# A hybrid encoder step whose inputs arrive in another host layout: key cache and memory tokens turned, weights contiguous per partition, states returned as they lie on chip

## The chip, the cores and the metric

The kernel runs on one core of a Trainium2 chip. TensorE (PE in the profile) multiplies, VectorE (DVE) and ScalarE (ACT) do the elementwise work, GpSimd (POOL) and SyncE (SP) issue most of the transfers. The metric is the device time of one execution in microseconds, lower is better.

## The reference, cut to what matters

One layer, fp32. A prompt of 512 positions and 8 cached samples of 16 positions (128 rows) go through the same weights.

```python
z = x @ w_in                       # [RG-LRU input | its gate | GLU | query | 3 branch gates]
xa_c = causal_depthwise_conv([conv_a_prev, xa])              # width 4
h, h_last = rg_lru(xa_c, h_prev, ...)                        # scan over positions
out_a = (h * gelu(ya)) @ proj_a
u = glu[..., :D_CONV] * sigmoid(glu[..., D_CONV:])
v = causal_depthwise_conv([conv_b_prev, u])                  # width 31
out_b = silu(layer_norm(v)) @ proj_b
out_c = mem_cross_attention(q, k, v) @ proj_c                # 4 heads, 256 memory tokens
merged = g0 * out_a + g1 * out_b + g2 * out_c
x = layer_norm(ALPHA * x + merged @ w_out)
x = layer_norm(ALPHA * x + swiglu(x))
```

For the prompt, `k` and `v` are `mem_prompt @ w_mem_k` and `mem_prompt @ w_mem_v`; for the samples they come from `cache_mem_k` and `cache_mem_v`. Besides the two results the kernel returns the new convolution and recurrence states and the new memory keys and values.

## The kernel before

All 640 rows are kept on chip with the model dimension on partitions (`xh`, `xl`), in two halves of 320 columns. Every fp32 product is made of three fp32r matmuls: each operand is split into a rounded high part and a low part, and high by high, high by low and low by high are summed. A weight block is loaded by SP into `wr` (1 MB, two buffers), ACT copies it to `wh` (high), DVE writes `wl` (low), and PE multiplies.

The program is a list of `Step`s in the order in which PE does them: keys and values of the memory tokens, GLU, query, RG-LRU input, gates and projections of branches C and B, RG-LRU gate, the gates of branch A (`Pair`, seven half-size products instead of eight, with the sums made on DVE and ACT), branch A's projection, `w_out`, the FFN and its down projection. Weights are prepared up to three steps ahead.

Between a step's matmuls the program advances `streams`: generators for the work beside the projections (attention, the convolutions, the recurrence). A stream goes on while the summed prices of DVE and ACT (`V.time`, `A.time`) are below that of PE (`P.time`), so the place of a stream's instructions follows from a table of prices; `finish` forces a stream to its end where a step needs it. The stream that multiplies the recurrence by its gate is `a_stream`; it copies each product to a rounded part on ACT and subtracts on DVE. Small tiles live in 52 slots (`s`), side results in two PSUM buffers (`pv`), projection sums in four (`pu`).

What the change touches before: `mem_turn` transposes the memory tokens on PE. `load_rows` loads 14 small arrays as rows, and `param_stream` turns them on PE into `pa` and `pb` (a parameter for each channel, on partitions) and the sample histories into `us`. `conv_b_states` turns the new state of convolution B back into rows, the end of `lru_stream` does it for `hout`. In `attn_sample`, `turn` transposes each of the 16 key cache tiles in eight blocks of eight, and ACT copies the result to `kt` for `scores`. Weight blocks are read with rows of 1 to 4 KB, a strided slice of the model's matrix. Nearly all compute instructions stand on line 64 in the profile, the line of the helper that records them; tile names tell them apart. Only the loop that runs the steps and the streams is needed to follow the order:

```python
for few in s.mm(s.w):
    ...
    advance()
    flush()
    while new:
        new.pop(0).prep_lo()
```

## Time and profile before

| | |
|---|---|
| median of three runs | 1083.74 us (1081.05 to 1085.24) |
| span of the profiled execution | 1078.8 us; the page has no device time of its own for it |
| PE / DVE / ACT / POOL busy | 98% / 74% / 44% / 10% |
| mean granted TensorE clock | 0.996 |
| read from and written to HBM | 112.41 MB, 9.61 MB |

A line of the page's groups gives engine, operation, result and operands by tile name, count, busy time and the mean of one; a row of the timeline gives start, length and the like, with the idle time of the engine just before it and what ended it in brackets. Matmuls are pipelined, so the length of a row on PE is longer than the time to the next start.

### The profile page before, as it was taken

The page shows a single profiled execution, that of the slowest core. Times are in us where ns is not written, and L with a number is a line of the kernel's source. Part 1 is how long each engine was busy: PE and PEld are TensorE (multiplying, and loading weights), DVE is VectorE, ACT ScalarE, POOL GpSimd, SP SyncE. Part 2 cuts the span into 40 slices and gives each one's busy share as a digit, 9 for nine tenths or more (in the row PEclk, how much of TensorE's full clock was granted, in tenths as well). Part 3 has the DMA queues.
Part 4 walks back from the last instruction along what each step waited for, and adds up shares of the span by engine and source line. Part 5 has one row for each costly group of instructions (what it writes and reads, how often), then busy time and mean ns, then how long its engine had stood idle before and what let it go on. Part 6 is the DMA issues. An engine that isn't in the chain of part 4 may idle for free.

```text
span 1078.8 us, 16991 instructions
## 1 busy us (share of the span) xinstructions
PE 1052.7 (98%) x6827; PEld 1002.7 (93%) x6827; DVE 798.6 (74%) x1357; ACT 479.4 (44%) x852; POOL 107.8 (10%) x158
## 2 busy tenths in 40 slices
PE   9799999999999999999999998999999999999997
PEld 8699999998999999999999888999999999888886
DVE  6939989988377747877545678888878887545775
ACT  5332655455584575455323024434444444343341
POOL 0300405325000000100001220000000000100111
PEclk9999999999999999999999999999999999999999
DMA  9822124625022122113326231222232222834481
GB/s 337 276 87 73 46 79 141 200 83 157 1 90 88 59 84 93 45 53 105 118 72 221 98 118 40 78 79 78 83 110 82 79 79 79 293 122 152 159 289 40
DMA packets 80334, 123.11 MB, mean 114 GB/s; under 512 B 4075, under 2 KB 59371, under 8 KB 80256
## 3 DMA queue, kind: packets, MB, share of 16 engines
q1 hardware_dynamic: 73168, 100.36, 28.3%
q0 software_dynamic: 7088, 21.68, 6.4%
q8 instruction: 53, 0.87, 0.3%
q14 instruction: 25, 0.20, 0.1%
HBM read 112.41 MB, written 9.61 MB: 113 GB/s over the span
## 4 chain that ended last, share of the span: by engine, by line
PE 54%; DVE 1%; ACT 0%; issue 0%; DVEq 0%; ACTq 0%
PE pu L64 48%; PE pv L64 6%; DVE s L64 1%; DVE xres L64 0%; ACT s L64 0%; ACT wh L64 0%; DVEq L1952 0%; ACT wl L64 0%; DVE st L64 0%; DVE mv L64 0%; DVE ve L64 0%; DVE wl L64 0%; ACTq L64 0%; DVEq L64 0%
## 5 line engine op out<-in xcount | busy, mean ns | idle before, releaser
L64 PE MATMUL pu<-xh,wh 128*128 128x320 f32 x1040 | 250.2, 313 | 7.4 <-ACT s L64 6.8
L64 PE MATMUL pu<-xh,wl 128*128 128x320 f32 x1040 | 245.9, 309 | 0.0
L64 ACT ACTIVATE wh<-wr 128x1024 fp32r<-128x1024 f32 (+1 forms) x149 | 135.2, 909 | 222.6 <-PE pu L64 137.7
L64 PE MATMUL pu<-xl,wh 128*128 128x320 f32 x888 | 218.9, 310 | 4.1 <-DVE xl L64 4.1
L64 PEld LDWEIGHTS pu<-xh,wh 128*128 128x128 f32 x1040 | 177.2, 189 | 11.0 <-ACT s L64 7.8
L64 PE MATMUL pu<-s,wh 128*128 128x320 f32 x1064 | 185.5, 310 | 0.9 <-DVE s L64 0.9
L64 PEld LDWEIGHTS pu<-xh,wl 128*128 128x128 f32 x1040 | 176.8, 188 | 0.0
L64 DVE TENSOR_TENSOR wl<-wr,wh 128x1024 fp32r<-128x1024 f32 (+1 forms) x113 | 130.1, 1152 | 62.6 <-ACT wh L64 62.5
L64 DVE TENSOR_TENSOR s<-s,s 128x640 fp32r<-128x640 f32 (+4 forms) x176 | 126.1, 733 | 66.9 <-ACT s L64 64.6
L64 PEld LDWEIGHTS pu<-s,wh 128*128 128x128 f32 x1064 | 163.4, 188 | 2.2 <-DVE s L64 2.0
L64 PEld LDWEIGHTS pu<-xl,wh 128*128 128x128 f32 x888 | 153.5, 188 | 4.7 <-DVE xl L64 4.7
L64 DVE TENSOR_TENSOR s<-s,pu 128x320 f32<-128x320 f32 x188 | 88.5, 485 | 84.5 <-PE pu L64 81.7
L64 PE MATMUL pu<-s,wl 128*128 128x320 f32 x808 | 147.0, 309 | 0.0
L64 ACT ACTIVATE s<-s 128x640 fp32r<-128x640 f32 (+4 forms) x144 | 87.7, 628 | 100.1 <-DVE s L64 99.5
L64 PEld LDWEIGHTS pu<-s,wl 128*128 128x128 f32 x808 | 126.0, 188 | 0.0
L64 PE MATMUL pu<-wh,s 128*128 128x512 f32 (+1 forms) x396 | 115.4, 383 | 0.1
L64 DVE SCALAR_TENSOR_TENSOR s<-s,pb,s 128x511 f32<-128x511 f32 (+14 forms) x240 | 112.6, 540 | 2.8 <-ACT s L64 2.8
L64 PEld LDWEIGHTS pu<-wh,s 128*128 128x128 f32 x396 | 72.5, 188 | 14.6 <-ACT wh L64 0.9
L64 ACT ACTIVATE s<-pu 128x320 f32<-128x320 f32 (+2 forms) x90 | 36.8, 444 | 66.9 <-PE pu L64 66.7
L64 PE MATMUL pu<-wl,s 128*128 128x512 f32 (+1 forms) x198 | 61.6, 383 | 1.9 <-DVE wl L64 1.9
L64 PE MATMUL pv<-wh,s 128*128 128x512 f32 (+1 forms) x152 | 48.7, 367 | 0.4 <-DVE xres L64 0.4
L64 PE MATMUL pv<-s,s 128*32 128x128 f32 (+4 forms) x420 | 45.8, 308 | 1.4 <-ACT s L64 1.4
(134 smaller groups left out, 1172.6 us busy)
## 6 DMA issues: line engine op xcount, KB each, us to landing
wr<-in_w_in SPq DMA_DIRECT2D x26, 1024.0 KB, 5.0
wr<-in_w_ffn_down SPq DMA_DIRECT2D x19, 1024.0 KB, 4.9
wr<-in_w_ffn_gate SPq DMA_DIRECT2D x11, 1024.0 KB, 5.3
wr<-in_w_ffn_up SPq DMA_DIRECT2D x11, 1024.0 KB, 5.4
s<-in_cache_mem_k POOLq DMA_DIRECT2D x16, 256.0 KB, 5.9
s<-in_cache_mem_v POOLq DMA_DIRECT2D x16, 256.0 KB, 4.5
wr<-in_proj_a SPq DMA_DIRECT2D x4, 1024.0 KB
wr<-in_w_out SPq DMA_DIRECT2D x4, 1024.0 KB, 5.8
```

The costliest lines, as they stand in the source:

```text
L64: return f(*a, **k)
```

## The change

The host lays out the arrays before they go to the device, and lays the results out again after it:

- Memory tokens arrive turned, in four tiles `[128, 2, 256]`; `mem_split` only splits them. 30 matmuls of the identity stand ahead of the first real one in place of 15.
- Parameters and small states arrive as `rows_a` and `rows_b`, already on partitions, and are loaded into `pa` and `pb`. The sample histories arrive as `hist_b`, with 16 empty columns, straight into `us`.
- The key cache arrives as `[head, 128, tokens]`, the value cache as one contiguous row for each partition; two heads of keys are loaded ahead.
- Weights arrive so that a block is one contiguous row for each partition.
- `us`, the last 30 columns of `up` and `hout` are stored as they lie on chip.

```diff
-def mem_turn(c):
-    p = pv()
-    for m in range(2):
-        for k in range(4):
-            P.transpose(p[:, m, k * 128:(k + 1) * 128], mem[m][c][:, k * 128:(k + 1) * 128], ident)
...
+def mem_split(i):
+    hi, lo = memT[i] = [get([128, 2, 256], F32R) for _ in range(2)]
+    split(hi, lo, mem[i])
+    free(mem[i])
...
-idle(5)
-mem_turn(0)
-idle(10)
+idle(15)
+mem_split(0)
+idle(15)
...
 def load_rows():
...
+    S.dma_start(pa, rows_a.rearrange("p (k r) -> p k r", k=KD))
+    S.dma_start(pb, rows_b.rearrange("p (k r) -> p k r", k=KC))
+        S.dma_start(us[k], hist_b[k].rearrange("p (b r) -> p b r", b=NB))
...
 def z_load(col, n=1):
...
-        zload[c] = Load([128, KD, 256],
-                        lambda c=c: w_in[:, c:c + 256].rearrange("(k p) n -> p k n", p=128), 2)
+        zload[c] = Load([128, 2, KD, 128],
+                        lambda c=c: blocks_of(w_in[c // 256], 2), 2)
...
 def conv_b_stream():
...
+        G.dma_start(state_b[k].rearrange("p (b r) -> p b r", b=NB), us[k])
+        G.dma_start(tail_b[k], up[k][:, TP - 30:TP])
         yield from conv_b_taps(k)
-        free(us[k])
...
-            yield from conv_b_states()
...
+        free(us[k], up[k])
...
 def attn_sample():
...
-            to[h] = [get([128, 4, 128]) for _ in range(4)]
-            rows = src[0].rearrange("b (m p) h d -> p (b m) h d", p=128)
+            to[h] = [get([128, 512]) for _ in range(4)]
             for i in range(4):
-                G.dma_start(to[h][i], rows[:, 4 * i:4 * i + 4, h])
+                G.dma_start(to[h][i], src[h][:, i * 512:(i + 1) * 512])
...
-        def turn(h, i):
...
-                    P.transpose(p[:, j, k * 128:(k + 1) * 128], kc[h][2 * i + j][:, k], ident)
...
+        for h in range(2):
+            load(kc, cache_k, h)
         yield None
         yield None
-        yield from room(2)
+        yield from room()
         acc = pv()
...
+        for h in range(NH):
+            yield None
+            scores(h)
+            if h + 2 < NH:
+                load(kc, cache_k, h + 2)
+            if h == NH - 1:
+                load(vc, cache_v, 0)
+            yield 1
...
 def lru_stream():
...
-            P.transpose(p[:36, j // 4, (j % 4) * 128:(j % 4 + 1) * 128], hout[:, j], ident)
...
+        G.dma_start(state_a.rearrange("p (k r) -> p k r", k=KD), hout)
```

The order of instructions changes at three places of note.

In the cached attention, PE's rows at the second head before: `ident` marks a transpose, `s_125` and `s_126` are tiles of the key cache, `s_129` to `s_132` turned copies, `s_95` the query.

```order
L64 MATMUL pu<-xl,wh 128x320 x2
L64 MATMUL pu<-xh,wl 128x320 x2
L64 MATMUL pv<-ident,s_125_2204 128x128 x4
L64 MATMUL pv<-ident,s_126_2205 128x128 x4
L64 MATMUL pv<-s_129_2249,s_95_1771 32x256
L64 MATMUL pv<-s_130_2251,s_95_1771 32x256
L64 MATMUL pv<-s_132_2302,s_95_1771 32x256
```

PE at the first head's scores now, with `s_113` to `s_116` tiles of the cache as loaded and `s_91` the query:

```order
L64 MATMUL pu<-xl,wh 128x320 x2
L64 MATMUL pu<-xh,wl 128x320 x2
L64 MATMUL pv<-s_113_2073,s_91_1756 32x256
L64 MATMUL pv<-s_114_2074,s_91_1756 32x256
L64 MATMUL pv<-s_115_2075,s_91_1756 32x256
L64 MATMUL pv<-s_116_2076,s_91_1756 32x256
```

The transposes are gone, and the scores read the loaded tile.

PE's first rows before, at the start of the program; `s_1` and `s_3` are memory tokens, `s_31` and `s_33` their rounded turned copies.

```order
L64 MATMUL pu<-ident 128x128 x5
L64 MATMUL pv<-ident,s_1_93 128x128 x4
L64 MATMUL pv<-ident,s_3_95 128x128 x4
L64 MATMUL pu<-ident 128x128 x10
L64 MATMUL pu<-wh,s_31_169 128x512
L64 MATMUL pu<-wh,s_33_173 128x512
```

PE's first rows now, with `s_31` and `s_41` rounded memory tiles and `s_32` a low part:

```order
L64 MATMUL pu<-ident 128x128 x30
L64 MATMUL pu<-wh,s_31_170 128x512 x4
L64 MATMUL pu<-wl,s_31_170 128x512 x4
L64 MATMUL pu<-wh,s_32_171 128x512 x4
L64 MATMUL pu<-wh,s_41_248 128x512 x4
```

Eight transposes ahead of the first real matmul and eight behind its step are gone; 15 identity matmuls have come.

DVE in the seven-product part of branch A's gates before; `wh<-` and `wl<-` are low halves of weights (both halves of a product's weights share a tile there), `s_320` and the like are sums of products.

```order
L64 TENSOR_TENSOR s_320_5251<-s_320_5251,pu 128x320
L64 TENSOR_TENSOR wh<-wr,wh 128x512
L64 TENSOR_TENSOR wl<-wr,wl 128x512
L64 TENSOR_TENSOR s_321_5252<-s_320_5251,pu 128x320
L64 TENSOR_TENSOR s_326_5293<-s_321_5252,pu 128x320
```

DVE at the same place now, where `s_248` is a rounded product of the recurrence with its gate and `s_251` the gate of the next one:

```order
L64 TENSOR_TENSOR s_282_5025<-s_282_5025,pu 128x320
L64 TENSOR_TENSOR wh<-wr,wh 128x512
L64 TENSOR_TENSOR s_249_4545<-s_183_3019,s_248_4544 128x640
L64 TENSOR_TENSOR wl<-wr,wl 128x512
L64 TENSOR_TENSOR s_189_3112<-s_189_3112,s_251_4581 128x640
```

Rows of `a_stream`, which stood ahead of this part, stand inside it; in all there are 14 of them up to the projection of branch A.

## The prediction

> **What bounds the kernel now.** I read the page's busy times first, then the busy times of stretches, then what TensorE (PE) waited for.

> ```profile
> PE 1052.7 (98%) x6827; PEld 1002.7 (93%) x6827; DVE 798.6 (74%) x1357; ACT 479.4 (44%) x852; POOL 107.8 (10%) x158
> PE 54%; DVE 1%; ACT 0%; issue 0%; DVEq 0%; ACTq 0%
> ...
> 21.10:38.00 16.90, 13.93 (x67) 10.55 (x66) 16.08 (x29) 8.78 (x15) 1.89 (x2) 1.00 0.82 271
> 38.00:56.50 18.50, 13.41 (x91) 12.37 (x89) 15.72 (x26) 5.24 (x9) 7.20 (x10) 1.00 0.85 283
> ...
> 62.80:160.00 97.20, 97.20 (x686) 97.18 (x685) 83.03 (x171) 45.30 (x113) 10.93 (x24) 1.00 0.22 71
> ...
> 191.80:230.70 38.90, 38.90 (x306) 36.41 (x304) 38.20 (x79) 19.89 (x43) 8.44 (x12) 1.00 0.58 173
> ...
> 477.00:527.00 50.00, 49.26 (x335) 49.26 (x336) 36.17 (x62) 27.27 (x49) 0.00 (x0) 1.00 0.31 97
> ```

> Each stretch gives its length and then the busy time of PE, weight loads, DVE, ACT and POOL. PE is busy for 98% of the span, and the share is not an average of unlike stages: from 62.8 to 160 it is 97.20 of 97.20. Only the opening differs. From 21.1 to 38 DVE is the full engine (16.08 of 16.90) and PE idles 3 us; from 38 to 56.5 PE idles 5.1. At 191.8 both are full; at 477 DVE has room.

> ```profile
> PE pu L64 <- ACT s L64: 6.8, 3, 4.3
> PE pu L64 <- DVE xl L64: 4.1, 2, 3.3
> PE pu L64 <- DVE wl L64: 1.9, 1, 1.9
> ...
> PE pv L64 <- DVE xl L64: 0.3, 1, 0.3
> 30.77 1.34 PE L64 MATMUL pu<-wl,s 128*128 128x512 f32 x4 [1.85 <-DVE wl L64]
> 41.66 0.42 PE L64 MATMUL pu<-xl,wh 128*128 128x320 f32 x1 [3.33 <-DVE xl L64]
> ```

> These are the first three and the last of the ten releasers that PE waited for; all ten are DVE or ACT, none a transfer. So a faster weight load by itself is worth nothing in PE's dense part, and an instruction taken off PE there is worth its spacing, as long as DVE and ACT keep up.

> **The change part by part: key cache.** 64 PE transposes go, and 16 ACT copies with them.

> ```profile
> 191.86 1.03 PE L64 MATMUL pv<-ident,s 128*128 128x128 f32 x8
> 192.65 0.54 PE L64 MATMUL pu<-xh,wh 128*128 128x320 f32 x2
> ...
> 195.96 0.45 PE L64 MATMUL pu<-xh,wl 128*128 128x320 f32 x2
> 196.25 1.04 PE L64 MATMUL pv<-ident,s 128*128 128x128 f32 x8
> 200.65 0.60 PE L64 MATMUL pv<-ident,s 128*128 128x128 f32 x4
> ```

> Between two blocks of eight transposes stand 24 projection matmuls. Their last pair takes 0.29 (195.96 to 196.25), 0.147 each, so 24 take 3.52; the blocks start 4.39 apart (191.86 to 196.25). A block therefore costs 0.87, or 0.109 a transpose. Eight blocks: **7.0 us**.

> PE's score matmuls now read the loaded tile itself (first pair of orders in the part on the change).

> **Parameter rows, histories and states.** 32 more transposes go from the dense part.

> ```profile
> 58.04 0.31 PE L64 MATMUL pu<-xh,wl 128*128 128x320 f32 x1
> 58.19 1.63 PE L64 MATMUL pv<-ident,s 86*128 86x86 f32 x8
> ...
> 60.00 0.31 PE L64 MATMUL pu<-xl,wh 128*128 128x320 f32 x1
> ...
> 61.46 0.32 PE L64 MATMUL pu<-xh,wl 128*128 128x320 f32 x1
> 61.62 0.99 PE L64 MATMUL pv<-ident,s 120*128 120x120 f32 x8
> ...
> 62.60 0.31 PE L64 MATMUL pu<-xl,wh 128*128 128x320 f32 x1
> L64 PE MATMUL pv<-ident,s 128*30 128x128 f32 x4 | 0.9, 273 | 0.0
> L64 PE MATMUL pv<-ident,hout x8: 270/272/273, 432.6 to 433.4; 128*36 128x128 f32 x8
> ```

> The row that is left out before 60.00 is one matmul, so 58.04 to 60.00 holds two spacings (0.29) and the parameter block: 1.67. 61.46 to 62.60 gives 0.85 for the convolution histories. The state rows of convolution B (4 of 30 columns and 4 of 128) are 8 transposes, those of `hout` another 8 at the same spacing (432.6 to 433.4 from first to last): 0.87 each. Together 4.3, and with the keys **11.2 us**. The 15 ACT copies and 25 small stores that go with them lie on engines with room (ACT 44%); the larger state stores run beside PE. Cost: nothing; if POOL's queue were needed at that moment, 0.5 to 0.75 an issue.

> **The opening.** 16 memory transposes go, 15 idle matmuls (two records each) come.

> ```profile
> 1.44 2.50 PE L64 MATMUL pu<-ident 128*128 128x128 f32 x10 [1.44 <-DVE ident L64]
> 3.74 1.91 PE L64 MATMUL pv<-ident,s 128*128 128x128 f32 x8
> 5.45 2.71 PE L64 MATMUL pu<-ident 128*128 128x128 f32 x20
> 8.21 1.26 PE L64 MATMUL pu<-wh,s 128*128 128x512 f32 x4
> ```

> By the second pair of orders, 60 records stand where 38 stood; 22 more at 0.109 put the first real matmul 2.4 later, near 10.6, and the second memory block gives 0.87 back. That is 1.5 late on PE, against 3.0 us in which PE waited for DVE from 21.1 to 38 and 5.1 after it. DVE's rows there are the same splits and norms in the same order, so the wait shrinks and the end stays: 0. The weight blocks arrive in longer rows now, and the DMA engines are busy for 0.82 and 0.85 of these two stretches; a transfer that lands earlier can only help where DVE stands idle, which is 0.82 (16.90 - 16.08) and 2.78 (18.50 - 15.72), 3.6 in all, and DVE's idle time there may as well be for ACT. Bounds: a loss of 2.4, or a gain of 0.87 and half of PE's 8.1 us of idle time (about the 3.6 of DVE); I take 0, nearest to the full DVE row.

> **Layout alone.** Contiguous rows for weights and values, two heads of keys ahead, and the histories with 16 empty columns change when a transfer lands, and no row of an engine. Behind the opening I cost them at nothing: what hides them is PE's own work, since no transfer is among its releasers, and at 62.8 to 160 the DMA engines are busy for 0.22, at 191.8 for 0.58. The histories and parameters are needed from 58 on, where the removed transposes read them; were they late, the convolution's stream would give its place to others and PE would go on. If that cover were gone, the price would be that of a late load (below, 4.4 each).

> **What is late next.** The scheduler fills DVE and ACT by its sum of PE time, which is now smaller, so recurrence work moves to later steps. In the gates of branch A, the part with seven products in place of eight (trace from 477), DVE now has rows of the recurrence between the low halves of the weights that PE waits for (third pair of orders). 14 such 128x640 rows moved into the 28 products.

> ```profile
> L64 DVE TENSOR_TENSOR s<-s,s 128x640 f32<-128x640 f32 x56 | 45.9, 820 | 1.7 <-ACT s L64 0.7
> L64 ACT ACTIVATE s<-s 128x640 fp32r<-128x640 f32 x64 | 46.3, 730 | 54.8 <-DVE s L64 54.8
> 476.11 0.74 ACT L64 ACTIVATE s<-s 128x640 fp32r<-128x640 f32 x1 [1.73 <-DVE s L64]
> 477.27 0.42 ACT L64 ACTIVATE s<-pu 128x320 f32<-128x320 f32 x1
> 477.74 0.42 PE L64 MATMUL pu<-xh,wh 128*128 128x320 f32 x1 [1.81 <-ACT s L64]
> ```

> 14 x 0.82 = 11.5 on top of 36.17 makes DVE 47.7 of 50 there: nearly full, not over. At 477 PE already waited 1.81, because ACT's evacuation stood behind a copy that waited for DVE. The last scans of the recurrence now stand just ahead of that place. New waits: between 0 and 6 (seven products of the recurrence, each holding DVE for an ACT copy of 0.73, is 5.1, and 1 at the entry); I take 2.

> **Sum.** 1078.8 - 11.2 + 2 = 1069.6 span. The page gives no device time for its execution; the median of the runs, 1083.74, lies 4.9 above the span, and I keep that: **1074.5**.

> [...] The durations here are alike (270 to 273 ns), but the rows at 191.86 show the starts 0.109 apart, and the spacing decides.

> **Rivals.**
> *DVE takes PE's place* in the seven-product part: all of the 6 us of new waits, and 1 to 2 more where DVE was full at 191.8. For it: 38.20 of 38.90 there. Against it: DVE's lead over PE.

> ```profile
> 198.10 1.21 DVE L64 TENSOR_TENSOR wl<-wr,wh 128x1024 fp32r<-128x1024 f32 x1
> 210.64 1.03 PE L64 MATMUL pv<-ident,s 128*128 128x128 f32 x8
> ```

> Counted in DVE's order, the row at 198.10 is the low half for the projection step that PE begins behind the block at 210.64. It is done at 199.3, 11 us ahead. Time: 1083.74 - 11.2 + 7.5 = 1080.

> *The opening shortens too*, since the memory tiles no longer pass through PE: half of the 8.1 us. Time: 1074.5 - 4 = 1070.5. Against it: DVE's 16.08 of 16.90.

> *A transpose holds PE for its whole duration*: 96 x 0.273 = 26.2, so 1057.5. The rows at 191.86 speak against it.

> *Slower: PE stands in front of a load.* Before, an ACT copy lay between the key tile and PE.

> ```profile
> L1066 POOL DMA_DIRECT2D s<-in_cache_mem_k x16: 749/749/806, 178.4 to 190.8; - x16
> DMA to landing us min/median/max: 3.4/5.9/8.4
> ```

> Heads 2 and 3 of keys and values are issued two rounds ahead, 2 x 3.52 = 7.0. Four issues of 0.75 and the longest landing make 11.4. If POOL came to the load only then, each would be 4.4 late, 17.6 for four, and the time 1083.74 - 11.2 + 17.6 = 1090. It decides once slots come free less than 11.4 before use. Against it: POOL had issued all keys by 190.8, before the first turn.

> That the change doesn't remove the transposes is excluded by the order's rows.

> **How the numbers follow.** Forecast 0.62 (own range 1071.5 to 1077.5), DVE 0.20, opening 0.12, whole durations 0.02, slower 0.04. A measurement of this kernel tells about 0.5% (5.4 us) from no change, so faster means under 1078.3: the forecast, the opening, the whole durations and a third of the DVE case, 0.82; within, the rest of that case, 0.14; slower 0.04. The range 1069.5 to 1080.5 leaves out the ends of the opening case, half of DVE's and both far ones.

> **What would show it.** Right: blocks gone from 58 and from 190 to 230; no new releaser over 3 us; the end of the opening near 56.5 still released by DVE. Wrong: PE waits with `wh` or `wl` from DVE between the gate projection's start and the branch A projection (the DVE case); PE releasers named after the caches (slower); first projection matmul well before 38 (opening).

## The result, and the profile after

| | before | changed |
|---|---|---|
| median | 1082.53 us (1081.05 to 1085.24, 4 runs) | 1073.88 us (1072.94 to 1074.25, 4 runs) |
| ratio | | 0.9916, 95% interval 0.99 to 0.9932 |
| span of the profiled execution | 1078.8 us | 1072.1 us |
| granted clock, mean | 0.996 | 0.991 |

The kernel became 8.65 us faster; the forecast was 1074.5. The lines below show that the forecast's largest term holds, and that its smaller ones are not those that made up the sum.

The page of the changed kernel, then the busy times of the same stretches (length, then PE, weight loads, DVE, ACT, POOL, and then the granted clock):

```profile
PE 1047.4 (98%) x6745; PEld 998.4 (93%) x6745; DVE 798.8 (75%) x1357; ACT 469.1 (44%) x823; POOL 89.5 (8%) x142
38.00:56.50 18.50, 15.43 (x88) 14.95 (x88) 13.75 (x22) 3.35 (x6) 1.86 (x2) 0.82 0.53 174
62.80:160.00 97.20, 94.75 (x654) 94.33 (x653) 78.93 (x157) 41.56 (x98) 10.58 (x30) 0.98 0.23 79
191.80:230.70 38.90, 38.66 (x320) 34.76 (x319) 32.01 (x65) 17.58 (x45) 7.79 (x15) 1.00 0.43 146
477.00:527.00 50.00, 50.00 (x342) 49.90 (x341) 43.62 (x71) 28.49 (x49) 0.00 (x0) 1.00 0.30 106
```

PE is busy 5.3 us less (1052.7 to 1047.4), where 11.2 were to go. Two clocks are new: 0.82 from 38 to 56.5 and 0.98 from 62.8 to 160, where before had 1.00. From 62.8 to 160 PE now also idles 2.45. At 477, where new waits were forecast, PE has none (50.00 of 50.00). From 191.8 on DVE, nearly full before (38.20 of 38.90), has 32.01 now. What PE waited for, and two places in its timeline:

```profile
PE pu L64 <- ACT s L64: 8.0, 5, 4.3
PE pu L64 <- DVE xl L64: 4.2, 2, 3.4
...
36.14 0.31 PE L64 MATMUL pu<-xh,wh 128*128 128x320 f32 x1
39.81 0.63 PE L64 MATMUL pu<-xl,wh 128*128 128x320 f32 x1 [3.35 <-DVE xl L64]
40.24 0.47 PE L64 MATMUL pu<-xh,wl 128*128 128x320 f32 x1
40.50 0.47 PE L64 MATMUL pu<-xh,wh 128*128 128x320 f32 x1
...
45.57 0.31 PE L64 MATMUL pu<-xl,wh 128*128 128x320 f32 x1
...
127.01 0.46 PE L64 MATMUL pu<-xh,wl 128*128 128x320 f32 x2
129.92 0.74 PE L64 MATMUL pu<-xh,wh 128*128 128x320 f32 x2 [2.45 <-ACT s L64]
```

The wait for `xl` ends at 39.81, 1.85 earlier than before (41.66). But the matmuls behind it start 0.26 apart until 45.57, and 0.15 apart from there. The granted clock of that stretch is 0.50, called half speed here, as these windows of both profiled executions show, first the changed kernel's, then before's:

```profile
35.30:38.72 3.42, 1.15 (x6) 0.69 (x4) 3.35 (x6) 2.60 (x5) 1.48 (x1) 1.00 0.79 302
38.73:42.14 3.41, 2.33 (x9) 2.34 (x10) 3.41 (x6) 0.45 (x1) 0.00 (x0) 0.50 0.53 113
42.14:45.55 3.41, 3.41 (x14) 3.41 (x14) 3.27 (x6) 0.00 (x0) 0.00 (x0) 0.50 0.97 318
127.47:130.88 3.41, 0.96 (x5) 0.82 (x6) 3.41 (x8) 3.38 (x8) 0.00 (x0) 1.00 0.00 0
130.89:134.29 3.40, 3.40 (x15) 3.40 (x14) 3.40 (x8) 1.83 (x5) 0.00 (x0) 0.50 0.00 0
666.78:670.19 3.41, 2.62 (x10) 2.62 (x11) 3.38 (x6) 1.78 (x4) 0.00 (x0) 0.50 0.00 0
670.20:673.60 3.40, 3.40 (x14) 3.40 (x14) 2.27 (x4) 1.99 (x4) 0.00 (x0) 0.50 0.00 0
...
36.80:40.21 3.41, 1.53 (x8) 0.98 (x6) 3.34 (x7) 2.21 (x5) 1.41 (x1) 1.00 0.92 291
40.22:43.62 3.40, 1.96 (x13) 1.96 (x14) 3.40 (x6) 0.84 (x1) 0.05 (x1) 1.00 0.78 277
675.10:678.50 3.40, 3.40 (x13) 3.40 (x14) 3.37 (x6) 0.92 (x2) 0.00 (x0) 0.50 0.00 0
```

The windows are 3.41 us long because the stretches at 0.50 are, once (130.89 to 134.29, and 675.10 to 678.50 before) or twice (38.73 to 45.55, 666.78 to 673.60). The place of before's first two is an estimate, 186 steps of 3.413 back from 675.10. In the changed kernel PE was busy for 1.15 of the window up to 38.72 and 0.96 of the one up to 130.88, and the window behind each has 0.50. Before, nearly the same wait (3.33) lies in two windows (PE busy 1.53 and 1.96), and the clock there is 1.00. Half of PE's busy time in windows at 0.50 is counted as lost: (2.33 + 3.41 + 3.40 + 2.62 + 3.40)/2 = 7.6 us now, 1.7 before. The starts give somewhat less: from 40.24 to 45.57 they lie 0.267 apart in place of 0.147, which makes the lost share 0.45.

This gives an account of the two profiled executions. Span: -6.7. PE's idle time: 26.1 (1078.8 - 1052.7) to 24.7, -1.4. Lost to half speed: +5.9. What is left, PE's work at full speed, is -6.7 + 1.4 - 5.9 = **-11.2** (the start, ahead of the clock's first record, counted as full speed). A second pair of executions, before_again and after_again below (spans 1080.7 and 1070.0), gives -10.7 + 1.8 - 0.4 = -9.3. Both hold the identity matmuls of the opening, which the term of 11.2 did not count. Counted from the first projection matmul on (38.03 before, 36.14 now), PE's work at full speed fell by 11.3 in the first pair and by 10.2 in the second: the term holds within about a microsecond.

### The profile page after: what moved, and what is told of

It is laid out like the page before. It is cut to its first block, busy times and chain, and to the rows that moved or that the text cites. A ratio compares the mean times of both kernels' runs of the same rounds, so it can differ in the third digit from the quotient of the medians.

```text
span 1072.1 us, 16734 instructions
## 1 busy us (share of the span) xinstructions
PE 1047.4 (98%) x6745; PEld 998.4 (93%) x6745; DVE 798.8 (75%) x1357; ACT 469.1 (44%) x823; POOL 89.5 (8%) x142
## 4 chain that ended last, share of the span: by engine, by line
PE 83%; DVE 10%; DMA 3%; ACT 2%; issue 1%; POOL 0%; SPq 0%; DVEq 0%; POOLq 0%; ACTq 0%
PE pu L64 74%; PE pv L64 10%; DVE s L64 7%; DVE wl L64 2%; ACT s L64 1%; DMA s<-in_w_mem_k 1%; DMA pb<-in_rows_b 1%; DMA s<-in_x_prompt 1%; DMA s<-in_w_mem_v 1%; DVE xres L64 0%; DVE xl L64 0%; ACT L64 0%; DVE mx L64 0%; POOL s L777 0%; DVE nm L64 0%
## 5 line engine op out<-in xcount | busy, mean ns | idle before, releaser
L64 PE MATMUL pu<-xh,wh 128*128 128x320 f32 x1040 | 251.7, 314 | 8.3 <-ACT s L64 7.5
L64 PE MATMUL pu<-xh,wl 128*128 128x320 f32 x1040 | 247.6, 310 | 0.0
L64 ACT ACTIVATE wh<-wr 128x1024 fp32r<-128x1024 f32 (+1 forms) x149 | 135.1, 908 | 242.2 <-PE pu L64 152.4
L64 PE MATMUL pu<-xl,wh 128*128 128x320 f32 x888 | 220.6, 312 | 4.2 <-DVE xl L64 4.2
L64 PEld LDWEIGHTS pu<-xh,wh 128*128 128x128 f32 x1040 | 178.8, 190 | 12.9 <-ACT s L64 9.2
L64 PE MATMUL pu<-s,wh 128*128 128x320 f32 x1064 | 185.6, 310 | 1.7 <-DVE s L64 1.3
L64 DVE TENSOR_TENSOR s<-s,s 128x640 fp32r<-128x640 f32 (+4 forms) x180 | 129.0, 732 | 67.3 <-ACT s L64 60.7
L64 PEld LDWEIGHTS pu<-xh,wl 128*128 128x128 f32 x1040 | 178.2, 189 | 0.0
L64 DVE TENSOR_TENSOR wl<-wr,wh 128x1024 fp32r<-128x1024 f32 (+1 forms) x113 | 129.9, 1151 | 62.9 <-ACT wh L64 62.7
L64 PEld LDWEIGHTS pu<-s,wh 128*128 128x128 f32 x1064 | 163.1, 188 | 3.3 <-ACT wh L64 1.1
L64 PEld LDWEIGHTS pu<-xl,wh 128*128 128x128 f32 x888 | 155.1, 190 | 4.8 <-DVE xl L64 4.7
L64 PE MATMUL pu<-s,wl 128*128 128x320 f32 x808 | 148.1, 311 | 0.2 <-DVE s L64 0.2
L64 DVE TENSOR_TENSOR s<-s,pu 128x320 f32<-128x320 f32 x188 | 88.5, 485 | 75.0 <-PE pu L64 71.4
L64 ACT ACTIVATE s<-s 128x640 fp32r<-128x640 f32 (+4 forms) x148 | 89.8, 627 | 99.0 <-DVE s L64 97.6
L64 PEld LDWEIGHTS pu<-s,wl 128*128 128x128 f32 x808 | 126.8, 190 | 0.5 <-ACT wh L64 0.5
L64 DVE SCALAR_TENSOR_TENSOR s<-s,pb,s 128x511 f32<-128x511 f32 (+14 forms) x240 | 114.5, 549 | 9.5 <-ACT s L64 9.4
L64 PE MATMUL pu<-wh,s 128*128 128x512 f32 (+1 forms) x396 | 114.8, 383 | 0.0
L64 PEld LDWEIGHTS pu<-wh,s 128*128 128x128 f32 x396 | 72.8, 188 | 13.9
L64 ACT ACTIVATE s<-pu 128x320 f32<-128x320 f32 (+2 forms) x90 | 36.6, 441 | 71.9 <-PE pu L64 71.9
L64 PE MATMUL pu<-wl,s 128*128 128x512 f32 (+1 forms) x198 | 61.6, 383 | 0.4 <-DVE wl L64 0.4
L64 PE MATMUL pv<-wh,s 128*128 128x512 f32 (+1 forms) x152 | 48.7, 367 | 0.4 <-DVE xres L64 0.4
L64 PE MATMUL pu<-s,s 128*128 128x512 f32 (+1 forms) x204 | 46.6, 380 | 0.0
```

What stands on the lines that cost most here:

```text
L64: return f(*a, **k)
```

## The experiments

All medians are beside runs of the kernel before on the same chip (medians 1083.07, 1083.19 and 1083.38 in the three sets).

| label | median, us | ratio to before, 95% interval |
|---|---|---|
| before_again | 1084.43 | 1.0013 (1.0004 to 1.0022) |
| after_again | 1074.03 | 0.9919 (0.9905 to 0.9933) |
| warm_both | 1070.40 | 0.9887 (0.9874 to 0.9901) |
| credit | 1066.35 | 0.9846 (0.9833 to 0.986) |
| credit_warm | 1062.51 | 0.9804 (0.979 to 0.9819) |
| keys_on_chip | 1079.89 | 0.9966 (0.9954 to 0.9978) |
| params_on_chip | 1071.32 | 0.9892 (0.9876 to 0.9908) |
| mem_on_chip | 1075.14 | 0.9933 (0.9917 to 0.9949) |
| idle15 | 1074.54 | 0.9916 (0.9901 to 0.993) |
| strided | 1074.08 | 0.9914 (0.9897 to 0.993) |
| keys_only | 1078.60 | 0.996 (0.9945 to 0.9975) |
| before_warm | 1081.68 | 0.9983 (0.997 to 0.9995) |

The first row is a kernel against itself, and its interval leaves out 1: 0.0013 is what such a ratio can be off, beyond its interval.

### Does half speed follow from the program, or from the run?

Both kernels were run once more, unedited, to choose between two accounts: in the one, called the clock theory in the expectations, the windows at 0.50 stand at other places in other runs of the same program; in its rival the program alone sets them.

> The kernel before, once more. [...] Rival (the windows follow from the program alone): every run at 0.996, and the half-speed stretches stand again at 675 and at the end only.

> The changed kernel, once more. Clock theory: 1072.5 to 1074.5, granted clock 0.991 to 0.995, the half-speed stretches not all at the same places as in the first profile (38.7, 130.9, 666.8). Rival (they follow from the program): the same three places, clock 0.991 in every run. By both the waits of 3.35 at 39.8, 2.45 at 129.9 and 4.32 at 667.6 stand again within 0.2 us.

The second execution of before, with the windows around its first wait and around the one at 477:

```profile
39.23:42.62 3.39, 1.14 (x8) 1.14 (x9) 3.39 (x6) 1.62 (x3) 0.86 (x1) 1.00 0.92 334
42.64:46.03 3.39, 3.39 (x14) 3.39 (x14) 3.25 (x5) 0.00 (x0) 0.00 (x0) 0.50 0.96 245
476.13:479.53 3.40, 1.58 (x11) 1.32 (x10) 3.20 (x6) 2.57 (x5) 0.00 (x0) 1.00 0.00 0
479.54:482.95 3.41, 3.41 (x15) 3.41 (x14) 3.32 (x6) 1.51 (x3) 0.00 (x0) 0.50 0.02 5
```

The same program, but the windows meet at another place (42.63, where 40.22 was estimated for the first execution), and here the one behind 1.14 of 3.39 busy has 0.50; at 477 one behind 1.58 of 3.40, 1.82 idle, has it too. So the program alone does not set the places, and the profile of before that the forecast was made from (clock 0.996) had less half speed than most: of the 54 runs of before in the three sets and in before_again, five have 0.996 or more. Of the 15 runs of before beside this set, the two at clock 0.997 took 1080.52 and 1081.24, the four at 0.992 that took longest 1083.07 to 1084.63. The changed kernel's nine runs all lie at 0.991 or 0.992, 0.9917 in the mean, before's fifteen 0.9935. 0.0018 of 1075 us, or some 2 us, is an estimate of what half speed takes back from the change on the average; with the mean of all 54 runs of before, 0.9929, it is 1.3. The first pair had 5.9, the second 0.4 (5.1 lost in before_again, 5.5 in after_again). A run of 1082.32 at 0.992 says that the mean clock alone does not set the time; the mean also takes in windows in which PE waits (busy for 2.33 of 3.41 at 38.73 in the changed kernel).

after_again came out nearer to the rival than to the clock theory. Its waits are the same (3.33, 2.43 and 4.32), its half-speed stretches follow the same three waits (from 39.52, 128.26 and 664.16), and no run left 0.991 to 0.992. Only the places of the windows differ: PE is busy for 3.03 and 2.90 of the first two half-speed windows, where it was busy for 2.33 of 3.41 and 3.40 of 3.40. So the mean clock of the changed kernel hardly differs between runs, and it is before's that does (0.992 to 0.997 in the fifteen). That waits of this length (2.43 to 4.32) are followed by half speed in most runs is the author's reading of these rows, not a test.

### Idle matmuls in the waits

The first loop stands ahead of the first projection step, the second ahead of the first seven-product step of the FFN. Both write a PSUM buffer that the next real product overwrites, and their price is not counted, so that the order stays.

```diff
+    for _ in range(14):
+        nc.tensor.matmul(q.p[0][:, :128], ident, ident, start=True, stop=True)
...
+    for _ in range(18):
+        nc.tensor.matmul(q[:, 0, :128], ident, ident, start=True, stop=True)
```

> 14 identity matmuls ahead of the first projection step and 18 ahead of the first seven-product step of the FFN, in the time in which PE waited 3.35 and 4.32 us. Clock theory: the half-speed stretches at 38.7 and 666.8 go, and with them (45.55 - 39.81)/2 = 2.9 and (673.6 - 667.6)/2 = 3.0; as DVE may be next at 55 the first is worth 2 to 2.9: 1068 to 1069.5, clock 0.997 or more. Rival (the waits alone cost time, DVE ends them at the same moment): no change against the changed kernel, 1073 to 1074.5. If the added matmuls delay what they stand ahead of: up to 1 slower.

> The kernel before with the 14 and 18 identity matmuls in its two long waits. Clock theory (half-speed stretches strike both kernels alike, in a part of the runs): 3 to 3.6 faster than before, 1079.5 to 1080, with a spread under 2 us where before has 4. Rival (only the changed kernel suffers from them): less than 1 faster, 1082 to 1083.

In the changed kernel: 3.6 us less than after_again, and PE's timeline there has no half speed behind the wait:

```profile
36.47 3.29 PE L687 MATMUL pu<-ident 128*128 128x128 f32 x28
39.51 0.39 PE L64 MATMUL pu<-xh,wh 128*128 128x320 f32 x1
40.14 0.41 PE L64 MATMUL pu<-xl,wh 128*128 128x320 f32 x1 [0.24 <-DVE xl L64]
40.40 0.31 PE L64 MATMUL pu<-xh,wl 128*128 128x320 f32 x1
40.54 0.31 PE L64 MATMUL pu<-xh,wh 128*128 128x320 f32 x1
```

From 40.40 on the starts lie 0.15 apart, where they lay 0.26 apart. The product that waits still comes when DVE has `xl` (40.14, 39.81 without); only what follows is quicker. In the kernel before the same edit gave 1.7 us, half of what was expected, and its runs spread over 4.9 (1079.05 to 1083.95) where under 2 was expected, so neither theory's number held. Its profile shows why part of it stayed away: two windows still have 0.50, at 479.75 (the wait at 477) and behind three short waits:

```profile
53.09:56.49 3.40, 1.64 (x11) 1.17 (x11) 1.03 (x3) 1.08 (x2) 0.67 (x2) 1.00 0.35 119
56.50:59.91 3.41, 3.41 (x14) 3.03 (x14) 0.41 (x1) 0.00 (x0) 0.00 (x0) 0.50 0.00 0
```

### Where the new wait of 2.45 comes from

ACT of the changed kernel, rows of the wait: `s<-pv,nm` are exponentials of the attention, `s<-pu` the evacuation that PE waits for.

```profile
127.54 0.48 ACT L64 ACTIVATE s<-pv,nm 128x256 f32<-128x256 f32 x1
128.13 1.28 ACT L64 ACT_TABLE_LOAD   x1
129.43 0.77 ACT L64 ACTIVATE s<-pu 128x320 f32<-128x320 f32 x2
```

The evacuation stands behind four exponentials and a table load. It did before, too, but there it began at 128.24, 1.3 us before PE ended its step and went on to a block of the attention:

```profile
128.24 0.77 ACT L64 ACTIVATE s<-pu 128x320 f32<-128x320 f32 x2
129.28 0.46 PE L64 MATMUL pu<-xh,wl 128*128 128x320 f32 x2
129.57 1.03 PE L64 MATMUL pv<-ident,s 128*128 128x128 f32 x8
130.36 1.67 PE L64 MATMUL pv<-s,s 128*128 128x256 f32 x12
131.87 0.46 PE L64 MATMUL pu<-xh,wh 128*128 128x320 f32 x2
```

In the changed kernel the attention has moved 24 projection matmuls on, its block to behind the step that waits, its exponentials on ACT with it. 24 at 0.147 are 3.5 us, and the evacuation now begins 2.0 after PE ended its step (127.47, which is 129.92 - 2.45) in place of 1.3 before it. So what PE lacks is not the block as a cover: before, the evacuation was done without it. What has changed is that the softmax stands on ACT in front of an evacuation that PE is about to need. If the place is the cause, it can be put back: by a credit in the sum of prices, or by undoing the part whose price had held the place.

```diff
         if i == first["q"] + 4:
+            P.time += 900
             streams.insert(0, ("attn", chain(attn_prompt(), attn_sample())))
```

> The changed kernel with 900 ns added once to the summed price of PE when the attention stream starts, which puts the blocks of the prompt's attention at the same projection matmuls as before (576 and 624, in place of 600 and 672). Theory (the new wait of 2.45 at 129.9 comes from the place of the softmax on ACT beside the evacuation of a projection): the wait goes or falls under 1, and the half-speed stretch behind it goes: 2 to 4 less than the changed kernel, 1070 to 1072. Rival (ACT and DVE are simply full there and PE came 2.25 us early): a wait of about the same size at the same or the next step, 1073 to 1074.5.

1066.35, 7.7 less, nearly twice the most that was expected; no wait is left there (129.35 follows the block at once):

```profile
127.05 1.03 PE L64 MATMUL pv<-ident,s 128*128 128x128 f32 x8
127.84 1.67 PE L64 MATMUL pv<-s,s 128*128 128x256 f32 x12
129.35 0.46 PE L64 MATMUL pu<-xh,wh 128*128 128x320 f32 x2
```

The other kernel, params_on_chip, turns the parameter rows and histories on PE again:

```diff
+            P.transpose(p[:, 0, k * 86:(k + 1) * 86], ra[:, k * 128:(k + 1) * 128], ident[:86, :86])
+            P.transpose(p[:, 1, k * 34:(k + 1) * 34], rb[0][:, k * 128:(k + 1) * 128], ident[:34, :34])
...
+                P.transpose(p[:, i, k * 120:(k + 1) * 120], rb[1 + i][:, k * 128:(k + 1) * 128], ident[:120, :120])
```

> The changed kernel with one part undone: parameter rows and the histories of convolution B arrive as rows, PE turns them in 16 transposes and ACT copies them (11 copies); the attention's blocks fall back to the projection matmuls 576 and 624 of before. The term alone: 2.5 slower than the changed kernel's 1074.0, 1076.5. Theory (the removal of just these transposes moved the attention by one place and brought the wait at 129 with its half-speed stretch, and the 7.7 of the credit is what that place costs): faster than the changed kernel in spite of the added work, 1074.0 + 2.5 - 7.7 = 1068.8. Rival (the credit gained by something else than the place): 1075 to 1077.

1071.32: with 16 transposes more than the changed kernel it is 2.7 us **faster**. It does not reach 1068.8. With the forecast's 2.5 for the transposes the place costs 2.7 + 2.5 = 5.2. This is an upper estimate: the four runs of params_on_chip have a clock of 0.995, and its profiled execution has no half-speed window at the opening, though the same wait stands there (3.34 at 40.46), so up to 1.7 of the 2.7, half a window of 3.41, may come from that. The wait of 2.45 and the window behind it alone make 4.1. The remaining 2.5 to 3.6 of the credit's 7.7 come from something else, in part perhaps from what it moved later on; its waits after 200 are other ones (1.05 at 295 and 0.97 at 467, in place of 0.84, 0.46, 0.43 and 0.53). Which move it was isn't settled.

### The parts, undone one by one

keys_on_chip: the cache arrives unturned and PE turns it as before.

```diff
+                    P.transpose(p[:, j, k * 128:(k + 1) * 128], kc[h][2 * i + j][:, k * 128:(k + 1) * 128], ident)
...
+                        copy(kt[-1], p[:, j])
```

> The changed kernel with one part undone: the key cache arrives unturned (contiguous rows), PE turns it in 64 transposes and ACT copies them. Forecast's term (0.109 each, 0.87 a block): 7.0 slower than the changed kernel's 1074.0, so 1081. Rival A (DVE is the bound there, 38.2 of 38.9 busy): 0 to 2 slower, 1074 to 1076. Rival B (a transpose holds PE for its 0.27): 17 slower, 1091. By all, the place of the attention stream may shift a step, and with it a wait of up to 2.5.

The same two matmuls in the two kernels, ahead of the turns and behind them, first the changed kernel:

```profile
161.15 0.39 PE L64 MATMUL pu<-xh,wh 128*128 128x320 f32 x1
329.18 0.31 PE L64 MATMUL pu<-s,wh 128*128 128x320 f32 x1
...
161.80 0.39 PE L64 MATMUL pu<-xh,wh 128*128 128x320 f32 x1
336.97 0.31 PE L64 MATMUL pu<-s,wh 128*128 128x320 f32 x1
```

168.03 and 175.17 between them: 7.14 for 64 transposes, of which 0.5 are longer waits of PE, so 0.104 each, where the forecast had 0.109. In the median of runs it is 5.9. The groups of the trace count 196 rows of `pv<-ident,s` with 273 ns each; at 273 the 64 would be 17, so the length of a row is again not what it costs here.

keys_only: the kernel before with `cache_mem_k` turned on the host and read as in the change, nothing else.

> The kernel before with the key cache alone turned on the host. The term alone: 7.0 faster than before, 1076.1. If the attention behind it packs better too (shorter waits between 239 and 300, which were 2.4 in sum before): up to 9.5 faster, 1073.6. If DVE bounds that part: 1078 or more.

1078.60, 4.8 faster (1083.38 before): less than the term. Its waits between 239 and 300 became shorter, but others came behind them (0.57 at 339, 0.85 at 480), and with the same 26.1 us of idle time its span is 1077.4. The number is the one named for DVE as the bound of that part, but DVE is busy for 31.88 of 38.90 there (38.20 before), so the reason is not shown by it. Its profiled execution also lost more to half speed, 4.5 (1.7 before). Removed from before, the transposes are worth less than they cost when they are put into the changed kernel. Which of the places that moved takes the rest wasn't tried.

idle15, strided and mem_on_chip take the opening apart.

```diff
-    idle(15)
-    mem_split(0)
-    idle(15)
+    idle(5)
+    mem_split(0)
+    idle(10)
```

> The changed kernel with 15 identity matmuls at the start as before (5 and 10), in place of 30. Forecast's step (DVE sets the end of the opening): no change, 1073 to 1075, the first real matmul about 3.3 us earlier and the wait in front of the first projection step longer by as much. Rival (PE's start is on the path, since DVE waits for nothing of PE any more): 1.5 to 3 faster, 1071 to 1072.5. [...]

The loads of `w_in` in strided; those of the other projections and of the FFN likewise:

```diff
-                            lambda c=c: blocks_of(w_in[c // 256], 2), 2)
+                            lambda c=c: w_in[:, c:c + 256].rearrange("(k p) n -> p k n", p=128), 2)
```

> The changed kernel with the weights of all projections and of the FFN read from the model's own layout, rows of 1 to 4 KB, as before; all else as changed. Forecast's step (no transfer releases PE): no change, 1073 to 1075. Rival (the 1.85 us that the opening became shorter come from faster loads): 1 to 2 slower, 1075 to 1076, with the wait at 39.8 released at 41 to 42.

```diff
+                P.transpose(p[:, m, k * 128:(k + 1) * 128], mem[m][c][:, k * 128:(k + 1) * 128], ident)
...
-    idle(15)
-    mem_split(0)
-    idle(15)
+    idle(5)
+    mem_turn(0)
+    idle(10)
```

> The changed kernel with the memory tokens turned on PE as before, and 15 identity matmuls. Forecast's step (the opening's end is DVE's and stays): 1073 to 1075. Rival (the opening became 1.85 shorter since DVE no longer waits for ACT's copies out of PSUM): the first wait for xl ends at 41.5 in place of 39.8, and the time is 1 to 2.5 slower, 1075 to 1076.5.

Where the wait for `xl` ends, in idle15, strided and mem_on_chip:

```profile
39.72 0.42 PE L64 MATMUL pu<-xl,wh 128*128 128x320 f32 x1 [2.85 <-DVE xl L64]
...
40.22 0.42 PE L64 MATMUL pu<-xl,wh 128*128 128x320 f32 x1 [3.33 <-DVE xl L64]
...
42.10 0.42 PE L64 MATMUL pu<-xl,wh 128*128 128x320 f32 x1 [3.32 <-DVE xl L64]
```

Neither the number of idle matmuls nor the layout of the weights moves it by more than 0.41; both kernels take the changed kernel's time (1074.54, 1074.08). With the memory tokens on PE again, and their loads in before's order, it ends 2.3 later and the time is 1.1 longer. DVE's rows in mem_on_chip show what it waits for there, ACT's copies out of PSUM; DVE in the changed kernel waits for no such copy.

```profile
13.31 0.69 DVE L64 TENSOR_TENSOR s<-pv,s 128x512 fp32r<-128x512 f32 x1 [0.44 <-ACT s L64]
14.66 0.69 DVE L64 TENSOR_TENSOR s<-pv,s 128x512 fp32r<-128x512 f32 x1 [0.67 <-ACT s L64]
```

These two waits are the smaller part. DVE's first split of the memory tokens, first below in before, starts at 4.19 in the changed kernel, 2.1 earlier. But there DVE then waits for a transfer, that of the first rows of `x_prompt`, second below:

```profile
6.32 0.69 DVE L64 TENSOR_TENSOR s<-pv,s 128x512 fp32r<-128x512 f32 x1 [4.93 <-ACT s L64]
8.60 1.38 DVE L64 BATCH_NORM_STATS2 st<-s 128x6 f32<-128x512 f32 x2 [2.22 <-DMA s<-in_x_prompt]
```

Between the end of these statistics and the end of the wait for `xl` lie 29.8 us in the changed kernel, after_again, idle15 and strided alike, and 30.9 in before, before_again and mem_on_chip. So the opening of the changed kernel now begins with a transfer, and the 0.41 of strided goes with a later landing of its second half (DVE's second row of statistics waits for it until 9.69). Whether loading `x_prompt` ahead of more of the memory tokens shortens it wasn't tried.

### Both gains together

credit_warm has the credit and the idle matmuls.

> The credit of 900 ns and the identity matmuls in both waits together. If the two gains are independent (7.7 and 3.6 below the changed kernel's 1074.0): 1062.7; the credit took a half-speed stretch at 128 that the identity matmuls don't touch, so nothing is counted twice. Rival (one takes the other's gain, since DVE bounds what follows the opening): 1064.5 to 1066. Only half-speed stretches at the end remain, clock 0.998.

1062.51 (1062.27 to 1062.62): the gains add, and it is the fastest of all kernels here, 20.7 us under before and 11.5 under the changed kernel. Its page:

```profile
PE 1046.4 (99%) x6809; PEld 999.3 (94%) x6809; DVE 799.8 (75%) x1357; ACT 467.0 (44%) x822; POOL 90.9 (9%) x142
```

The granted clock of its runs is 0.998 or 0.999, and they spread over 0.35 us where before's spread over 4. The small spread alone does not show that the half-speed windows are gone, for credit's runs spread over 0.32 at a clock of 0.994; the clock shows it.

## Why the prediction came out right, step by step

1. *Key cache, -7.0.* Right, with its reason: 7.14 by the trace of keys_on_chip, 6.6 without the longer waits. The rival in which a transpose holds PE for its whole duration is excluded, and so is the one in which PE stands in front of the cache loads (no releaser of the changed kernel is a cache transfer). *DVE takes PE's place* did not come either: PE is busy for 50.00 of 50.00 from 477 on, and DVE for 32.01 of 38.90 from 191.8 on.
2. *Parameter rows and histories, -2.5; states -1.7.* The size is right: params_on_chip has the two blocks on PE again (1.62 and 0.98 long in its timeline), and PE's work at full speed behind the opening fell by 11.3 and 10.2 in the two pairs, keys included. What the step left out is the price that went with them: params_on_chip is 2.7 faster with the parameter part on PE, mainly since removing it had moved the attention.
3. *New waits, +2, at 477.* The size of one was right and the place wrong. The wait at 477 shrank:

```profile
469.75 0.41 PE L64 MATMUL pu<-xh,wh 128*128 128x320 f32 x1 [0.53 <-ACT s L64]
```

DVE took the rows that moved there (43.62 of 50 busy, where 47.7 was forecast and 36.17 stood before) without holding PE up. The new wait of 2.45 came at 129.92, in a stretch that the forecast had called dense, and behind ACT, not DVE; that its size is near the 2 forecast for another place is luck. Failed step: "The scheduler fills DVE and ACT by its sum of PE time, which is now smaller" was followed for the recurrence alone; the attention, which hangs on the same sum, was not.

4. *Opening, 0.* The wait ends 1.85 earlier: the rival "the opening shortens too" had the mechanism, and its counter-argument (DVE full with the same rows) failed, for the rows were the same but DVE starts on them 2.1 earlier and no longer waits for ACT's later copies; a wait for `x_prompt` took part of that back. The first real matmul came 1.4 later in place of 2.4 (8.21 to 9.65), with no effect on the end. In the first profile the gain was given back behind the wait by half speed, (2.33 + 3.41)/2 = 2.9.
5. *Half speed.* In no term. 5.9 between the first two profiled executions, 0.4 between the second two, 1.3 to 2 between the runs by estimate.
6. *4.9 around the span.* The run that was profiled took 1074.25 for a span of 1072.1, so what lies around it is 2.15. By the same 2.15 before's profiled execution took some 1081, so the rest of the 4.9 was that it was faster than the median; that it had a single half-speed window in PE's work fits this. Taken as an offset, the rest carried the missing step 5 into the sum by chance.

So the sum of 1074.5 is right by its largest terms, 1 and 2. That it is only 0.6 off is luck: the span was forecast 2.5 too low (1069.6, measured 1072.1) and the offset 3.1 too high (4.9, measured 1.8 to the median), and 4 and 5 were missed with opposite signs.

## What to carry to other kernels

Price a transpose on a full PE by the distance of the starts around it, and test it by putting it back, which gave 0.10 us here. Where the order follows a sum of prices, removing cheap work can move a block of other work, whose rows on another engine then stand in front of a result that PE needs: before believing a gain or a loss, put the place back with the work still gone. Where a kernel's runs spread more than its measurement should, look at the granted clock behind each wait of PE; filling the waits with idle matmuls was worth 3.6 us here (1.7 in the kernel before), and it can be read off only when several executions are compared.

## What the runs showed of the hardware

| execution | window up to | its clock | PE busy | clock of the next |
|---|---|---|---|---|
| changed | 38.72 | 1.00 | 1.15 of 3.42 | 0.50 |
| changed | 130.88 | 1.00 | 0.96 of 3.41 | 0.50 |
| before, second | 42.62 | 1.00 | 1.14 of 3.39 | 0.50 |
| before, second | 479.53 | 1.00 | 1.58 of 3.40 | 0.50 |
| before_warm | 56.49 | 1.00 | 1.64 of 3.40 | 0.50 |
| before, first | 40.21 | 1.00 | 1.53 of 3.41 | 1.00 |
| before, first | 43.62 | 1.00 | 1.96 of 3.40 | 1.00 |
| changed | 42.14 | 0.50 | 2.33 of 3.41 | 0.50 |
| changed | 670.19 | 0.50 | 2.62 of 3.41 | 0.50 |
| changed | 45.55 | 0.50 | 3.41 of 3.41 | 1.00 |
| changed | 134.29 | 0.50 | 3.40 of 3.40 | 1.00 |

The 1.82 us without PE in the fourth row and three waits of 0.27, 0.69 and 0.80 together in the fifth stand ahead of a window at 0.50; the sixth row, with less of PE than either, does not. Its place is the estimate from above, and the ends of PE's rows are modelled, so these rows give no bound on the busy share.
